# A two-layer backbone on one core: six output blocks with the contraction outside, elementwise work off GpSimd, and new figures for the scheduler

## The chip, the core and the metric

The kernel runs on one core of a Trainium2 chip. A core has a matrix engine (TensorE, PE in the rows), a vector engine (VectorE, DVE), an activation engine (ScalarE, ACT), a general engine (GpSimd, POOL) and a queue engine (SyncE, SP), which here only starts transfers. SBUF is the memory on the core, PSUM its accumulators. The metric is device time in microseconds: the median of repeated executions of the whole program. Shares of time, waits and the clock granted to TensorE (1.0 is 2.4 GHz, 0.5 is 1.2 GHz) come from one profiled execution.

## The reference, cut

Two layers work on 256 latent and 256 context tokens, all float32. `c` gives a modulation of nine vectors for each layer, by one matrix product each.

```python
def swiglu(h, w_gate, w_up, w_down):
    return (jax.nn.silu(h @ w_gate) * (h @ w_up)) @ w_down
def sublayer_in(h, g_pre, mod, s):
    return rmsnorm(h, g_pre) * (1 + mod[:, 3 * s + 1]) + mod[:, 3 * s]
def sublayer_out(h, y, g_post, mod, s, weight):
    return h + weight * mod[:, 3 * s + 2] * rmsnorm(y, g_post)
...
for l in range(DEPTH):
    mod_x = (silu_c @ ada_w[l] + ada_b[l]).reshape(B, N_ADA, 1, D_MODEL)
    mod_c = (silu_cc @ ada_w[l] + ada_b[l]).reshape(1, N_ADA, 1, D_MODEL)
    y = swiglu(sublayer_in(x, norm_pre[l, 0], mod_x, 0), ffn_w_gate[l, 0], ffn_w_up[l, 0], ffn_w_down[l, 0])
    x = sublayer_out(x, y, norm_post[l, 0], mod_x, 0, FFN_RESIDUAL_WEIGHT)
    ...  # the same for ctx; then the mixer (attention and a state space model), then a second FFN
```

The model width is 1024, the FFN's inner width 2816. The last FFN is run for the latent tokens alone.

## The kernel before, in words

**Layout.** Activations lie with channels on the 128 partitions: eight blocks of 128 channels by 512 columns, of which half (h = 0) are context and half (h = 1) latent tokens. Each float32 product is made of three matmuls at the fast rate: weights and activations are split into a high and a low part (`whi`, `wlo`; `hhi`, `hlo`), and high x high, high x low and low x high are added in PSUM (`mm3`). A weight tile `raw` of 128x512 is loaded by SP, its high part made by ACT, its low part by DVE.

**The opening.** `run` loads x, then takes the first two modulation vectors in four quarters (`ada_first`): eight loads `aw` of 256 KB for each quarter, 32 narrow matmuls into 32 partitions, an evacuation `adr` by ACT, a transposition and three small steps on DVE that give the coefficients of two channel blocks. Squares of x go through ones-matmuls into the bank `misc`; `chain` makes the inverse root for each half (rows `rs` of 64 columns on DVE, `sp` the masked rows of 256 columns that a matmul spreads over all partitions). `block` normalises a half of a channel block: `pn` on DVE, `hhi` and again `pn` on ACT, `hlo` on DVE. Then `lead` runs the first six output blocks (three gate/up pairs) for the half h = 0, pair by pair over all eight contraction blocks, and then for h = 1, with 256 columns a matmul. All later blocks have 512 columns.

**Norm changes.** There are five more: FFN to mixer, mixer to FFN and FFN to the next layer's FFN, and the two of layer 1. Each closes the old sublayer (`close`: squares, and the product x times y, together in the tile `tri`, summed by ones-matmuls), makes the factors (`chain`, twice: for the old norm and the new one), and for each block forms `po` = y times the old factor, the sum of x and po, `pn`, `hhi` and `hlo`. Most products `tri` and most sums of x and po run on GpSimd. At the last change (`xonly`, 256 columns, new tiles `xn`) GpSimd also makes the first mask and the products of the first two blocks (EARLY), which read a copy of the factor in SBUF (`b1`).

**What sets the order.** The program records all instructions and a list scheduler orders them before the build: each has a key (the planned TensorE time of the main work before it, plus or minus a shift), a planned duration (`cost`), and a pull towards its kind (TABLE and TILE price a change of ACT's table or TensorE's tile shape). Work aside from the main line (the modulation's rest, the state space model's tables `mt`, `P` and others on DVE) is spread by a pace: PACE_A and PACE_B planned nanoseconds of key for one of DVE. Every instruction is recorded by one helper, so all stand on one line (L576 before, L582 after), and rows are told apart by their tiles.

## Time and profile before

| what | value |
|---|---|
| median of 3 runs | 2302.32 us (2298.68 to 2303.83) |
| profiled execution, its own time | 2301.47 us |
| its span in the trace | 2299.7 us |
| busy: PE, DVE, ACT, POOL | 97%, 81%, 45%, 13% |
| granted clock over the span | 0.988 |
| transfers | 428.06 MB, 186 GB/s on average |

The span is the time between the first and the last instruction of the trace; the execution's own time has 1.8 us more around it. TensorE is nearly always busy, so what counts is where it is not, and where it works at half its clock. An average over the whole run hides this: the table in windows shows it.

### The profile page before, as it was taken

The page shows a single profiled execution, that of the slowest core. Times are in us where ns is not written, and L with a number is a line of the kernel's source. Part 1 is how long each engine was busy: PE and PEld are TensorE (multiplying, and loading weights), DVE is VectorE, ACT ScalarE, POOL GpSimd, SP SyncE. Part 2 cuts the span into 40 slices and gives each one's busy share as a digit, 9 for nine tenths or more (in the row PEclk, how much of TensorE's full clock was granted, in tenths as well). Part 3 has the DMA queues.
Part 4 walks back from the last instruction along what each step waited for, and adds up shares of the span by engine and source line. Part 5 has one row for each costly group of instructions (what it writes and reads, how often), then busy time and mean ns, then how long its engine had stood idle before and what let it go on. Part 6 is the DMA issues. An engine that isn't in the chain of part 4 may idle for free.

```text
span 2299.7 us, 43776 instructions
## 1 busy us (share of the span) xinstructions
PE 2236.4 (97%) x15768; PEld 1926.3 (84%) x15768; DVE 1870.4 (81%) x4314; ACT 1034.4 (45%) x2050; POOL 297.0 (13%) x455
## 2 busy tenths in 40 slices
PE   8999999899999999999999989999999998998998
PEld 6888778787888888888888878888888897997997
DVE  4997878979989889699997999888557579886454
ACT  5332233653347644543222453333246446675452
POOL 0010011330100300200100231110003110312000
PEclk9999999999999999999999989999999999998999
DMA  9344556954975556133554644566444695773552
GB/s 312 102 163 137 172 203 205 359 199 154 319 260 172 170 163 217 48 128 117 176 183 139 210 148 158 200 213 220 152 147 150 236 319 179 186 258 111 179 193 87
DMA packets 237481, 428.06 MB, mean 186 GB/s; under 512 B 29488, under 2 KB 58032, under 8 KB 237264
## 3 DMA queue, kind: packets, MB, share of 16 engines
q1 hardware_dynamic: 213904, 350.79, 47.2%
q0 software_dynamic: 23360, 74.48, 9.2%
q8 instruction: 124, 2.03, 0.4%
q14 instruction: 93, 0.76, 0.1%
HBM read 366.56 MB, written 58.59 MB: 185 GB/s over the span
## 4 chain that ended last, share of the span: by engine, by line
PE 75%; DVE 8%; DMA 3%; issue 1%; ACT 1%; POOL 0%; DVEq 0%; SPq 0%; ACTq 0%; POOLq 0%
PE acc L576 74%; DVE rs L576 1%; DVE t L576 1%; DVE wlo L576 1%; DMA aw<-in_ada_w_dram 1%; PE misc L576 1%; DVE lo L576 1%; DVE w L576 1%; DMA ar<-in_ada_t_dram 0%; DMA m1l<-stg 0%; DMA raw<-in_w_in_dram 0%; DVE po L576 0%; DVE hlo L576 0%; DVE X L576 0%; DVE sp L576 0%
## 5 line engine op out<-in xcount | busy, mean ns | idle before, releaser
L576 PE MATMUL acc<-hhi,whi 128*128 128x256 f32 (+2 forms) x2112 | 717.8, 345 | 5.1 <-ACT hhi L576 4.2
L576 PE MATMUL acc<-hlo,whi 128*128 128x256 f32 (+2 forms) x2112 | 703.9, 344 | 4.8 <-DVE hlo L576 4.8
L576 PE MATMUL acc<-hhi,wlo 128*128 128x256 f32 (+2 forms) x2112 | 706.3, 343 | 0.5 <-DVE wlo L576 0.2
L576 ACT ACTIVATE whi<-raw 128x512 fp32r<-128x512 f32 x802 | 479.0, 624 | 366.7 <-PE acc L576 141.3
L576 DVE TENSOR_TENSOR wlo<-raw,whi 128x512 fp32r<-128x512 f32 x802 | 530.1, 689 | 133.1 <-ACT whi L576 80.3
L576 PEld LDWEIGHTS acc<-hhi,whi 128*128 128x128 f32 (+1 forms) x2112 | 398.7, 190 | 57.2 <-ACT hhi L576 7.0
L576 PEld LDWEIGHTS acc<-hhi,wlo 128*128 128x128 f32 (+1 forms) x2112 | 399.0, 190 | 49.4 <-DVE wlo L576 2.8
L576 PEld LDWEIGHTS acc<-hlo,whi 128*128 128x128 f32 (+1 forms) x2112 | 392.3, 190 | 55.2 <-DVE hlo L576 7.7
L576 PE MATMUL acc<-hi,whi 128*128 128x512 f32 (+1 forms) x1144 | 390.7, 344 | 2.4 <-DVE lo L576 2.0
L576 PE MATMUL acc<-lo,whi 128*128 128x512 f32 (+1 forms) x1144 | 388.6, 341 | 0.0
L576 PE MATMUL acc<-hi,wlo 128*128 128x512 f32 (+1 forms) x1144 | 384.2, 343 | 1.0 <-DVE wlo L576 1.0
L576 PEld LDWEIGHTS acc<-hi,whi 128*128 128x128 f32 x1144 | 215.3, 189 | 32.3 <-DVE lo L576 2.4
L576 PEld LDWEIGHTS acc<-hi,wlo 128*128 128x128 f32 x1144 | 214.4, 189 | 27.8 <-DVE wlo L576 2.2
L576 PEld LDWEIGHTS acc<-lo,whi 128*128 128x128 f32 x1144 | 215.5, 189 | 25.0 <-issue 0.9
L576 ACT ACTIVATE sg<-acc 128x512 f32<-128x512 f32 (+1 forms) x129 | 64.9, 504 | 231.5 <-PE acc L576 212.9
L576 ACT ACTIVATE hi<-sg 128x512 fp32r<-128x512 f32 (+1 forms) x113 | 60.6, 542 | 167.9 <-DVE sg L576 142.2
L576 DVE TENSOR_TENSOR sg<-sg,acc 128x512 f32<-128x512 f32 (+1 forms) x97 | 55.7, 575 | 97.0 <-ACT sg L576 62.0
L576 POOL TENSOR_TENSOR tri<-x,y 128x256 f32<-128x256 f32 x54 | 52.4, 976 | 320.5 <-ACT y L576 299.0
L576 POOL DMA_DIRECT2D stg<-P x64 | 34.8, 543 | 376.7 <-DVE P L576 360.9
L576 DVE CUSTOM_DVE_ANT_0 ar<-ar,crow,adab 128x512 f32<-128x512 f32 x104 | 79.0, 760 | 3.6 <-DMA ar<-in_ada_t_dram 3.4
L576 DVE CUSTOM_DVE_ANT_0 ar<-ar,crow,ah 128x512 f32<-128x512 f32 x104 | 79.0, 759 | 2.0 <-DMA ar<-in_ada_t_dram 1.1
L576 DVE TENSOR_TENSOR lo<-sg,hi 128x512 fp32r<-128x512 f32 (+1 forms) x113 | 65.6, 586 | 16.9 <-ACT hi L576 10.8
(249 smaller groups left out, 3234.5 us busy)
## 6 DMA issues: line engine op xcount, KB each, us to landing
raw<-in_w_gu_dram SPq DMA_DIRECT2D x352, 256.0 KB, 3.2
ar<-in_ada_t_dram SPq DMA_DIRECT2D x208, 256.0 KB, 3.5
raw<-in_w_dn_dram SPq DMA_DIRECT2D x176, 256.0 KB, 3.1
raw<-in_w_sq_dram SPq DMA_DIRECT2D x128, 256.0 KB, 4.3
raw<-in_w_in_dram SPq DMA_DIRECT2D x112, 256.0 KB, 5.2
m1l<-stg SPq DMA_DIRECT2D x96, 256.0 KB, 5.1
aw<-in_ada_w_dram SPq DMA_DIRECT2D x80, 256.0 KB, 5.8
stg<-P POOLq DMA_DIRECT2D x64, 256.0 KB, 3.4
```

The lines of the kernel that those rows point to most:

```text
L576: getattr(getattr(self.tc.nc, engine), method)(*[real(v) for v in a], **{k: real(v) for k, v in kw.items()})
```

## The change

- The first FFN of layer 0 gets its own `lead_first`: all six blocks are open at once, in six banks; for each quarter of the modulation the two channel blocks are normalised in both halves, and each of them runs through all six blocks with 512 columns a matmul. The weights come in halves: the six for contraction blocks 0 to 3 ahead of quarter 0, the other six ahead of quarter 2. `with self.rec.at(...)` gives loads a fixed key (FIRST for the modulation's quarters, FIRST_W for the weights), which sets SP's order.
- The inverse root of both halves is made in one go of 128 columns (`open`), into one bank; `keep` copies both factors to SBUF after the first quarter. The transposition of a quarter uses the other part of that quarter's bank.
- No product or sum is left on GpSimd: `tri`, the sums, the last change's products and mask are DVE's. The copy `b1` and EARLY go. GpSimd keeps its transfers and small clears.
- Planned durations change: matmuls, the scan, a transfer started by GpSimd, its landing, TILE from 90 to 180. PACE_B goes from 2.5 to 3.2.

```diff
-PACE_A, PACE_B = 1.6, 2.5
+PACE_A, PACE_B = 1.6, 3.2
...
-FIRST = (5000, 1000, 1000, 1000)
+FIRST, FIRST_W = (1, 3, 4, 6), (2, 5)
...
-    TABLE, TILE = 1283, 90
+    TABLE, TILE = 1283, 180
...
-            return 1038 if eng == "POOL" else 525
+            return 545 if eng == "POOL" else 525
...
-            if m < 128:
-                return 28 + max(n, m) * passes * m / 307.2
-            return 2.5 + max(n * passes / 2.4, 53.3 * min(passes, 2) * (1 if method == "transpose" else 2))
+            if m < 128 and passes > 1:
+                return 6 + n * passes * m / 307.2
+            return (13.5 if passes == 1 else 4) + n * passes / 2.4
...
+        if method == "tensor_tensor_scan":
+            return 67 + 2.083 * n
...
-                    dma = max(dma, op.end + self.DMA_IN + 1000 * (e == "POOL")) + op.bytes / 360.0
+                    dma = max(dma, op.end + self.DMA_IN + 1400 * (e == "POOL")) + op.bytes / 360.0
...
-            nc.gpsimd.tensor_tensor(xy, x, y, op=ALU.mult)
+            nc.vector.tensor_tensor(xy, x, y, op=ALU.mult)
...
+    def lead_first(self, nrm, evac, first):
+        nc = self.nc
+        mine = self.chunks[self.i_get:self.i_get + 2 * LEAD]
...
+        bank, ws = [], [[None, None] for _ in range(LEAD)]
+        next(first)
+        for q in range(4):
+            if q % 2 == 0:
+                for i in range(LEAD):
+                    r = self.rec.tile("slot", 512, F32, "raw")
+                    with self.rec.at(FIRST_W[q // 2]):
+                        nc.sync.dma_start(r, mine[2 * i + q // 2][0])
+                    ws[i][q // 2] = r
+            with self.rec.ahead(URGENT):
+                for k in (2 * q, 2 * q + 1):
+                    self.rec.urgent = k == 0
+                    for h in (0, 1):
+                        nrm.block(h, k)
+            self.rec.urgent = False
+            if q == 0:
+                nrm.keep()
+            for k in (2 * q, 2 * q + 1):
+                for i in range(LEAD):
+                    if k == 0:
+                        bank.append(self.acc())
+                    if k % 4 == 0:
+                        ws[i][q // 2] = self.split(ws[i][q // 2], 512, self.blk(512, F32R, "whi"),
+                                                   self.blk(512, F32R, "wlo"))
+                    self.mm3(bank[i], ws[i], k, nrm.h[k], k == 0, k == NB - 1)
+                if k % 2 == 0:
+                    next(first, None)
+        for j in range(LEAD // 2):
+            evac(j, bank[2 * j], bank[2 * j + 1])
...
-            e.tensor_tensor(t, T.part(self.y[i], h), b1, op=ALU.mult)
-            (nc.vector if i < 2 and not self.xonly else nc.gpsimd).tensor_tensor(xv, xo, t, op=ALU.add)
+            nc.vector.tensor_tensor(t, T.part(self.y[i], h), b1, op=ALU.mult)
+            nc.vector.tensor_tensor(xv, xo, t, op=ALU.add)
```

Two places show the new order. The first is TensorE in the opening, at its first weight matmuls: `aw` are the modulation's loads, `hhi` and `hlo` the parts of a normalised channel block, `whi` and `wlo` those of a weight tile, each `acc` a bank. Before:

```order
L576 MATMUL acc_392<-aw_289,c_70 32x128 x4
L576 MATMUL acc_429<-hhi_413,whi_357 128x256
L576 MATMUL acc_429<-hhi_413,wlo_373 128x256
L576 MATMUL acc_429<-hhi_413,whi_377 128x256
L576 MATMUL acc_429<-hhi_413,wlo_383 128x256
L576 MATMUL acc_392<-aw_299,c_70 32x128 x4
L576 MATMUL acc_392<-aw_315,c_70 32x128 x4
L576 MATMUL acc_429<-hlo_440,whi_357 128x256
```

And after, at the change from the second to the third quarter:

```order
L582 MATMUL acc_485<-hhi_539,wlo_487 128x512
L582 MATMUL acc_625<-aw_356,c_70 32x128 x4
L582 MATMUL acc_625<-aw_367,c_70 32x128 x4
L582 MATMUL acc_625<-aw_372,c_70 32x128 x4
L582 MATMUL acc_625<-aw_380,c_70 32x128 x4
L582 MATMUL acc_625<-aw_386,c_70 32x128 x4
L582 MATMUL acc_625<-aw_391,c_70 32x128 x4
L582 MATMUL acc_625<-aw_399,c_70 32x128 x4
L582 MATMUL acc_625<-aw_407,c_70 32x128 x4
L582 MATMUL acc_397<-hhi_557,whi_343 128x512
L582 MATMUL acc_397<-hlo_579,whi_343 128x512
```

The modulation's narrow matmuls stood between those of one pair of blocks; now a quarter's 32 stand together, between two channel blocks that each go through six banks.

The second place is DVE at the last norm change, from the last masked rows `sp` on. Before:

```order
L576 SCALAR_TENSOR_TENSOR sp_25539<-rs_25544,sp_25539 128x256
L576 TENSOR_TENSOR po_25550<-y_25234,acc_25519 128x256
L576 TENSOR_TENSOR po_25554<-y_25279,acc_25519 128x256
L576 TENSOR_TENSOR po_25558<-y_25346,acc_25519 128x256
L576 TENSOR_TENSOR pn_25560<-xn_25542,acc_25552 128x256
L576 TENSOR_TENSOR pn_25564<-xn_25547,acc_25552 128x256
```

After:

```order
L582 SCALAR_TENSOR_TENSOR sp_25341<-rs_25344,sp_25341 128x256
L582 TENSOR_TENSOR po_25348<-y_24976,acc_25327 128x256
L582 TENSOR_TENSOR po_25352<-y_25014,acc_25327 128x256
L582 TENSOR_TENSOR xn_25354<-x_84,po_25348 128x256
L582 TENSOR_TENSOR xn_25356<-x_85,po_25352 128x256
L582 TENSOR_TENSOR pn_25358<-xn_25354,acc_25350 128x256
L582 TENSOR_TENSOR pn_25360<-xn_25356,acc_25350 128x256
```

The products of the third to fifth block stood between `sp` and the first `pn`; now the products and sums of the first two blocks stand there, which GpSimd had made beside the chain.

## Rows read from the trace of the kernel before

**Rows 1.** The page, busy time of each engine, share of the span, instructions:

```profile
PE 2236.4 (97%) x15768; PEld 1926.3 (84%) x15768; DVE 1870.4 (81%) x4314; ACT 1034.4 (45%) x2050; POOL 297.0 (13%) x455
```

**Rows 2.** Windows of the opening: length; PE, PEld, DVE, ACT, POOL busy; PEclk, DMA, GB/s:

```profile
10.00:15.00 5.00, 3.94 (x104) 2.00 (x96) 1.19 (x11) 2.82 (x9) 0.00 (x0) 1.00 1.08 369
...
20.00:25.00 5.00, 4.16 (x45) 2.12 (x44) 4.97 (x17) 2.79 (x6) 0.00 (x0) 0.50 1.10 348
25.00:30.00 5.00, 5.00 (x57) 3.27 (x52) 0.69 (x4) 0.88 (x2) 0.00 (x0) 0.73 1.09 356
...
60.00:65.00 5.00, 5.00 (x43) 5.00 (x43) 4.93 (x15) 3.12 (x7) 0.00 (x0) 1.00 0.28 93
```

**Rows 3.** Timeline of PE in the opening: start, time, instruction and its count:

```profile
22.98 0.58 PE L576 MATMUL acc<-hhi,whi 128*128 128x256 f32 x1
...
43.39 1.08 PE L576 MATMUL acc<-aw,c 128*32 128x128 f32 x32
...
70.85 0.39 PE L576 MATMUL acc<-hlo,whi 128*128 128x512 f32 x1
```

**Rows 4.** Timeline of SP, which starts the transfers:

```profile
0.74 0.94 SPq L576 DMA_DIRECT2D aw<-in_ada_w_dram  x2
1.74 0.46 SPq L576 DMA_DIRECT2D cvec<-in_cvec_dram  x1
...
3.19 3.75 SPq L576 DMA_DIRECT2D x<-in_x_dram  x8
```

**Rows 5.** Timeline of ACT in the opening, with the idle time before and its releaser:

```profile
6.82 1.39 ACT L576 ACTIVATE sq<-x 128x256 f32<-128x256 f32 x4 [0.43 <-DMA x<-in_x_dram]
...
46.47 0.59 ACT L576 ACTIVATE hhi<-pn,c,cA 128x256 fp32r<-128x256 f32 x1
```

**Rows 6.** Windows of 50 us over the whole run, columns as in rows 2:

```profile
400.00:450.00 50.00, 45.85 (x605) 39.74 (x594) 46.28 (x102) 32.51 (x72) 20.20 (x33) 1.00 1.02 386
450.00:500.00 50.00, 47.01 (x403) 43.41 (x402) 49.46 (x143) 33.20 (x72) 16.69 (x23) 1.00 0.49 152
...
1350.00:1400.00 50.00, 44.68 (x333) 41.81 (x334) 47.91 (x125) 27.64 (x57) 13.55 (x20) 0.90 0.34 116
...
1600.00:1650.00 50.00, 50.00 (x222) 41.42 (x221) 28.67 (x60) 13.88 (x24) 0.00 (x0) 1.00 0.49 162
...
2050.00:2100.00 50.00, 40.40 (x354) 37.37 (x353) 40.24 (x95) 31.02 (x69) 17.32 (x15) 0.89 0.50 160
```

**Rows 7.** Groups of POOL: shapes, count, busy us and mean ns, idle before and releasers:

```profile
L576 POOL TENSOR_TENSOR tri<-x,y 128x256 f32<-128x256 f32 x54 | 52.4, 976 | 320.5 <-ACT y L576 299.0 <-PE misc L576 7.0 <-issue 6.7
L576 POOL TENSOR_TENSOR x<-x,po 128x256 f32<-128x256 f32 x48 | 40.8, 863 | 64.1 <-DVE po L576 59.5 <-ACT y L576 4.2
```

**Rows 8.** Timelines of DVE, then POOL, at the last norm change:

```profile
2087.98 0.23 DVE L576 TENSOR_TENSOR rs<-rs 128x64 f32<-128x64 f32 x1
2088.24 0.49 DVE L576 SCALAR_TENSOR_TENSOR rs<-rs,rs 128x64 f32<-128x64 f32 x2
...
2092.29 0.98 DVE L576 SCALAR_TENSOR_TENSOR rs<-rs,rs 128x64 f32<-128x64 f32 x2
2093.30 0.65 DVE L576 TENSOR_TENSOR rs<-rs 128x64 f32<-128x64 f32 x1
2093.87 0.95 DVE L576 TENSOR_TENSOR sp<-rs,ident 128x256 f32<-128x256 f32 x1
2094.75 0.73 DVE L576 TENSOR_TENSOR rs<-rs,rs 128x64 f32<-128x64 f32 x1
...
2096.35 1.07 DVE L576 TENSOR_TENSOR po<-y,acc 128x256 f32<-128x256 f32 x3
...
2092.46 1.41 POOL L576 TENSOR_TENSOR po<-y,b 128x256 f32<-128x256 f32 x2 [3.00 <-ACT b L576]
```

**Rows 9.** Groups of DVE, columns as in rows 7:

```profile
L576 DVE TENSOR_TENSOR hlo<-pn,hhi 128x256 fp32r<-128x256 f32 x88 | 40.8, 468 | 4.8 <-ACT pn L576 4.5
...
L576 DVE TENSOR_TENSOR pn<-x,acc 128x256 f32<-128x256 f32 x80 | 31.4, 412 | 6.7 <-ACT pn L576 4.2 <-PE acc L576 2.3
```

More of the change, by code (lines that the diff above doesn't have):

```diff
@@ L272, in ahead, with at @@
         return self.aside(-ns)
+    def at(self, key):
+        return self.aside(key - self.now - self.shift)
     def cost(self, eng, method, a, kw):
@@ L717, in stat, with rsqrt @@
             self.nc.tensor.matmul(out, self.ones, q[:, :, j], start=False, stop=False, skip_group_check=True)
-    def rsqrt(self, v, plain=False, wide=True, times=1.0, mask=None):
+    def rsqrt(self, v, plain=False, wide=True, times=1.0):
         nc = self.nc
         end = 1.875 * times
-        mask = mask or nc.vector
         n = v.shape[-1]
@@ L735, in rsqrt @@
             r = self.blk(256, name="sp").rearrange("p (j k) -> p j k", j=4)
-            mask.tensor_tensor(r, y[:, c:c + 64].unsqueeze(1).to_broadcast([128, 4, 64]), diagonal, op=ALU.mult)
+            nc.vector.tensor_tensor(r, y[:, c:c + 64].unsqueeze(1).to_broadcast([128, 4, 64]), diagonal, op=ALU.mult)
             rows.append(r)
@@ L842, in ada_first @@
         for q in range(4):
-            bank = self.acc()[:, 0:128]
+            full = self.acc()
+            bank = full[:, 0:128]
+            self.rec.pull = FIRST_PULL
             for kt in range(8):
@@ L846, in ada_first @@
                 src = self.io["ada_w"][0, kt * 128:(kt + 1) * 128, 0:2048].rearrange("p (m c) -> p m c", m=2)
-                with self.rec.ahead(FIRST[q]):
+                with self.rec.at(FIRST[q]):
                     nc.sync.dma_start(w.rearrange("p (m c) -> p m c", m=2), src[:, :, q * 256:q * 256 + 256])
@@ L854, in ada_first @@
             nc.scalar.activation(row, bank, AF.Copy)
-            tp = self.aux()[:, 0:128]
+            tp = full[:, 128:256]
             nc.tensor.transpose(tp, row, self.ident)
@@ L955, in gated, with ffn @@
         nc.vector.tensor_tensor(out[1], sg, _f(out[0]), op=ALU.subtract)
-    def ffn(self, l, f, nrm, nxt):
+    def ffn(self, l, f, nrm, nxt, first=None):
         nc = self.nc
@@ L964, in ffn, with evac @@
         g = {}
-        self.lead(nrm, self.gate_half(g, n))
+        if first is None:
+            self.lead(nrm, self.gate_half(g, n))
+        else:
+            def evac(j, pg, pu):
+                g[j] = self.blk(n, F32R, "hi"), self.blk(n, F32R, "lo")
+                self.gated(self.blk(n, name="sg"), pg, pu, g[j])
+            self.lead_first(nrm, evac, first)
         hh = nrm.h
@@ L1944, in run @@
         nc.vector.memset(self.ones, 1.0)
-        self.ve = [self.const([128, 64], name="ve") for _ in range(2)]
+        ve = self.const([128, 128], name="ve")
+        self.ve = [ve[:, 64 * h:64 * h + 64] for h in range(2)]
         self.mods = [self.const([128, 144]) for _ in range(L)]
@@ L1979, in run @@
             nc.vector.memset(self.region(3 * h), 0.0)
-            nrm.chain(h)
-        for _ in first:
-            pass
+        nrm.open(ve)
         self.rot = ld([128, 128], io["rot"], "rot")
@@ L2010, in to_next @@
                 return Norm(self, (l, 2), (l + 1, 0), y, False)
-            nrm = self.ffn(l, 0, nrm, to_mixer)
+            nrm = self.ffn(l, 0, nrm, to_mixer, first if l == 0 else None)
             nrm = self.mixer(l, xo, nrm, to_ffn2)
@@ L2045, in chain @@
         T.rec.urgent = self.xonly or RUSH
-        mask = T.nc.gpsimd if self.xonly else None
         b1, b2 = self.banks()
         self.bc[h] = T.flat(b1), T.flat(b2)
-        if self.post is not None:
-            w = T.blk(64, name="rs")
-            v.tensor_scalar(w, T.region(3 * h), D * EPS, None, op0=ALU.add)
-            st = T.region(3 * h + 1, 2)
-            if not self.xonly:
-                st = T.blk(128, name="rs")
-                v.tensor_copy(st, T.region(3 * h + 1, 2))
-                v.memset(T.region(3 * h, 3), 0.0)
-            r, rows = T.rsqrt(w, True, times=D ** 0.5, mask=mask)
-            T.spread(b1, rows[0])
-            if self.xonly:
-                self.b1 = T.flat(T.blk(256, name="b1"))
-                T.nc.scalar.activation(self.b1, T.flat(b1), AF.Copy)
-            a = T.blk(64, name="rs")
-            v.tensor_tensor(a, r, st[:, 0:64], op=ALU.mult)
-            v.scalar_tensor_tensor(a, st[:, 64:128], 2.0, a, op0=ALU.mult, op1=ALU.add)
-            v.tensor_tensor(a, a, r, op=ALU.mult)
-            v.tensor_tensor(T.ve[h], T.ve[h], a, op=ALU.add)
+        w = T.blk(64, name="rs")
+        v.tensor_scalar(w, T.region(3 * h), D * EPS, None, op0=ALU.add)
+        st = T.region(3 * h + 1, 2)
+        if not self.xonly:
+            st = T.blk(128, name="rs")
+            v.tensor_copy(st, T.region(3 * h + 1, 2))
+            v.memset(T.region(3 * h, 3), 0.0)
+        r, rows = T.rsqrt(w, True, times=D ** 0.5)
+        T.spread(b1, rows[0])
+        a = T.blk(64, name="rs")
+        v.tensor_tensor(a, r, st[:, 0:64], op=ALU.mult)
+        v.scalar_tensor_tensor(a, st[:, 64:128], 2.0, a, op0=ALU.mult, op1=ALU.add)
+        v.tensor_tensor(a, a, r, op=ALU.mult)
+        v.tensor_tensor(T.ve[h], T.ve[h], a, op=ALU.add)
         w = T.blk(64, name="rs")
@@ L2070, in chain, with open, keep @@
         T.rec.urgent = False
+    def open(self, ve):
+        T = self.T
+        T.rec.urgent = True
+        bank = T.acc()
+        w = T.blk(128, name="rs")
+        T.nc.vector.tensor_scalar(w, ve, D * EPS, None, op0=ALU.max)
+        for h, r in enumerate(T.rsqrt(w, times=D ** 0.5)[1]):
+            T.spread(bank[:, 256 * h:256 * h + 256], r)
+            self.bc[h] = None, T.flat(bank[:, 256 * h:256 * h + 256])
+        T.rec.urgent = False
+    def keep(self):
+        for h in range(2):
+            b = self.T.flat(self.T.blk(256, name="fb"))
+            self.T.nc.scalar.activation(b, self.bc[h][1], AF.Copy)
+            self.bc[h] = None, b
     def block(self, h, i):
```

11 lines of the change are left out of this document (7 added, 4 removed).

## The prediction

> **What bounds the kernel now.** I began with the page's busy shares: TensorE is busy for 2236.4 of 2299.7 us [rows 1], so 63.3 us of idle time are all that a better order can win, beside stretches in which it works at a low granted clock and beside the work itself. Then the table in windows of 50 us [rows 6]: a steady stretch shows 222 matmuls of 512 columns in 50.00 us, 0.2252 us each, with nothing idle. The idle time sits at the opening and at the changes from one norm to the next: 4.2 and 3.0 us between 400 and 500, 5.3 between 1350 and 1400, 9.6 between 2050 and 2100. In the first three of these windows DVE is busy for 46.28 to 49.46 of 50 us: there DVE is late, not TensorE. The reader is to see in the opening's windows [rows 2] that the DMA engines are full (a share of 1.08 to 1.10, 348 to 369 GB/s) while TensorE waits or runs at half speed: a granted clock of 0.50 from 20 to 25 us and 0.73 from 25 to 30, so in these ten microseconds 3.9 us are lost to the clock alone. TensorE's own rows [rows 3] give the ends of the opening: the first weight matmul at 22.98 us, the first 512-column one, with which the first six output blocks are over, at 70.85.
>
> **The opening.** Before, the six blocks are 288 matmuls of 256 columns; 43 of these stand in 5 us at full clock [rows 2], 0.116 us each, 33.5 us. Now they are 144 of 512 columns, 144 x 0.2252 = 32.4 us: 1.1 us of pure work is gone. More is in when they may run. The order rows show that each quarter of the contraction now feeds all six blocks and both halves of the columns as soon as a quarter of the modulation is there, where before the first half of the columns ran through all eight contraction blocks and the second half followed.
>
> The transfers set one floor. Ahead of the last quarter's matmuls stand 8 of x, 32 of the modulation's weights and 12 halves of the first six blocks, 52 transfers of 256 KB. At 360 GB/s [rows 2] one takes 0.73 us. The loads of x now follow three small ones; these took 1.74 to 3.19 us before, 1.45 us, so x is issued from about 2.2 us instead of 3.19 [rows 4]. The first one was in use 3.6 us after its issue [rows 4, 5], so now at 5.8, and the 52nd lands at 5.8 + 51 x 0.73 = 43.0. From the last of these matmuls to the first normalised block it took 43.39 to 46.47, 3.1 us [rows 3, 5]; two more activations and the second half's pass are some 1.2 us; then 36 matmuls of 0.2252 us, 8.1. Floor by transfers: 55.4 us.
>
> TensorE sets the other. Its first weight matmul needs the same 16 transfers (x and one quarter) and the same chain as before, so it starts at about 22.5, near the 22.98 of before. From there: 32.4 us of weight matmuls; three quarters of the modulation, 96 matmuls, of which 32 took 1.08 us [rows 3], 3.2 us; and the 3.9 us of low clock, which I leave as they are, since the first quarter still waits for weights to be split. That is 62.0. The same sum for before, 22.98 + 33.5 + 3.2 + 3.9 = 63.6, falls 7.3 us short of the 70.85 measured; the rest was waits and changes between narrow and wide matmuls. Now the modulation's matmuls stand in solid groups, so I expect a fifth of that rest, 1.5 us, and take 63.5: **7.3 us** gained. The bounds are 55.4 (15.4 gained) and 62.0 + 7.3 = 69.3 (1.5 gained). I take a value near TensorE's own sum because it is the later of the two floors. What comes next is a steady stretch of 512-column matmuls at full occupation, so the gain is carried on, up to the next place where DVE is late.
>
> The copy of the row factors to SBUF (two activations) lies on ACT while it waits for data, and frees a bank; I cost it at nothing. One thing may be late: on ACT the evacuation of the last quarter's modulation now stands behind an exponential's table load and splits of three later weight tiles. These tiles are some 7 transfers further, 5 us, so the evacuation may slip to about 49 us; TensorE then still has the third quarter's matmuls to run. Without that cover it would cost up to 5 us, which is inside the bounds.
>
> **GpSimd's arithmetic on DVE.** 54 products tri and 48 sums x leave GpSimd, where one took 0.98 and 0.86 us [rows 7], and with them, at the last norm change, 8 sums, 2 products and a mask (so many by the code): 113 instructions. On DVE three such products in a row took 1.07 us for the first 0.41 and two more [rows 8], 0.33 us each, so DVE gets 37.7 us more, about 8 at each of the first four norm changes and 5 to 6 at the last. Against it stands what GpSimd takes from DVE while it runs. In the last norm change two products of 64 columns took 0.49 us when GpSimd was idle and 0.98 while it multiplied; single products of 64 columns took 0.65 and 0.73 there and the mask of 256 columns 0.95, against 0.23 and some 0.41 undisturbed [rows 8]: 0.49 + 0.42 + 0.50 + 0.54 makes 1.9 us lost in a chain on which TensorE waits, while GpSimd did its two products and the two sums behind them. Over the whole run the same is seen in the mean: the subtraction hlo, of the same size as pn but with both inputs in SBUF, took 468 ns against 412 [rows 9]. So 113 instructions off GpSimd give DVE back between nothing and 113 x 0.48 = 54 us (1.9 us by four instructions); I take 34, near the rows of the chain but with the tri products, which run beside PSUM work, giving less. DVE's load at a norm change then grows by 0 to 3 us, while each link that went through GpSimd gets 0.4 to 0.6 us shorter.
>
> At the last norm change the chain is urgent and nothing else is on DVE, so nearly all of the 1.9 us comes off directly; the mask that GpSimd had made beside it costs 0.1 of it. The products and sums of the first two blocks now stand on DVE, 4 x 0.33 = 1.3 us, in the gap between the second factor's rows (sp) and the first pn, in which DVE already did three products of 1.07 us [rows 8]; hence **1.8 us** gained, bounds 0 and 4 (the second with the low clock that such a wait leaves). At the other four I take **3 us** in all, bounds 12 lost and 11 gained (half of the 22 us of idle time in the three worst windows and the last).
>
> Here a rule speaks against the change. The Trainium skill, "Perfetto Trace Analysis", section "Optimizing Scalar/DVE Operations", says that with DVE saturated, moving work to other engines, even GpSimd, may make sense, and adds that the two share a read port, so that it might not help. The change goes the other way at stretches where DVE is saturated. By the first half of the rule the norm changes get longer (the third rival); rows 8 side with the second half.
>
> **The scheduler's figures.** The planned cost of a 512-column matmul rises from 215.9 to 226.8 ns, against 225.2 measured [rows 6]; the planned cost of a DMA issue on GpSimd falls to the measured size. Work that is due by planned TensorE time (the state space model's tables on DVE) so comes about 5% earlier against TensorE's true time, and what of it piled up on DVE at 400 us is smaller. PACE_B of 3.2 thins the same work in layer 1. I put no separate gain on this; it is why the 3 us above are not a loss. All else is a new order of equal work, worth between -5 and +5 us.
>
> **Sum.** The profiled execution took 2301.47 us, 0.85 below the median of 2302.32, so no correction: 2301.5 - 7.3 - 1.8 - 3.0 = 2289.4, **2289 us**.
>
> **Rivals.**
> 1. *More is freed.* The opening comes down near the transfers' floor (12 us) and the norm changes lose half of their idle time (11) with the clock they waste (3): 2301.5 - 26 = 2275. For it: those windows wait on DVE rows that GpSimd slowed. Against it: DVE is busy for 49.46 of 50 us from 450 on [rows 6] and sheds nothing. Chance 0.17.
> 2. *The clock takes the opening's gain.* Between quarters TensorE now waits for the next quarter's data. If the clock falls to 1.2 GHz at each wait, as in 20 to 25 us [rows 2], the first two quarters (16 us at full clock) need up to 16 us more; half of it eats the 7.3, and 2297 to 2301 remain. Against it: by the sums above TensorE is the later one from 30 us on, so it does not wait. The Trainium skill, "TensorE: Matmul & The Clock Gate", section "HAM oscillation — how this bites in real kernels", describes a kernel that falls back to the low clock at every contraction tile since each tile's data is waited for. No row here shows it after 30 us. Chance 0.15 together with other ways to stay within 0.2%: DVE's new load giving back what the opening gave (2302).
> 3. *DVE becomes later: slower.* If GpSimd's absence gives DVE little back, each saturated norm change (400 to 500, 1300 to 1400) grows by its 24 x 0.33 = 8 us, the two others by half: 24 us. Less 7.3 and 1.8: 2301.5 + 14.9 = 2316. It decides against the change from where less than 24 of the 37.7 us come back. Rows 8 show more coming back than is added (0.48 us for 0.33 an instruction). Chance 0.09.
>
> **How the numbers follow.** About 0.2% is what a measurement of this kernel can tell from no change, 4.6 us: faster means under 2297.7, slower over 2306.9. The forecast (2281 to 2297) has 0.59, rival 1 0.17, rivals 2 and 3 0.15 and 0.09. Faster 0.77, same 0.14, slower 0.09; 0.01 of rival 2 lies below its limit. The range reaches to rival 1's time and to no change: 2274 to 2302. It leaves out 0.09 of rival 3, about 0.05 of rival 2 and about 0.05 of rival 1.
>
> **What would show it.** The first 512-column matmul of the seventh block at 61 to 66 us; granted clock 1.0 from 30 us on; DVE's hlo at about 415 ns and its 64-column rows at 0.23 us in every norm change; the last wait on sp shorter by 1.8 us; TensorE idle in 400 to 500 at or under 7 us. Wrong would be: the seventh block after 68 us, TensorE waiting longer on DVE around 400 and 1350, or a new wait on weights where DVE's splits come late.

## The result, and the profile after

The changed kernel takes **2273.74 us** (median of 4 runs, 2269.72 to 2279.49), the kernel before 2300.5 beside it (4 runs, 2296.01 to 2303.83): a ratio of 0.9889, 95% interval 0.9876 to 0.9901, so 26.8 us less. The forecast was 2289, with a range that began at 2274: right in direction, less than half of the gain, and just outside the range. The profiled execution of the changed kernel is the slowest of its four (2279.49), so the two traces are 22.0 us apart and not 26.8.

The page of the changed kernel, busy time (against [rows 1]):

```profile
PE 2226.1 (98%) x15624; PEld 1909.5 (84%) x15624; DVE 1872.8 (82%) x4412; ACT 1031.5 (45%) x2045; POOL 195.7 (9%) x342
```

DVE is busy for 2.4 us more than before, near the prediction's account (37.7 added, 34 given back). GpSimd has lost 101 us, and TensorE's idle time fell from 63.3 to 51.6 us.

Windows of the changed kernel, columns as in [rows 2] and [rows 6] (busy time of each engine and, in brackets, its instructions):

```profile
20.00:25.00 5.00, 1.20 (x3) 0.92 (x4) 3.99 (x13) 3.96 (x10) 0.00 (x0) 0.86 1.04 342
25.00:30.00 5.00, 5.00 (x32) 2.62 (x32) 5.00 (x13) 3.61 (x8) 0.00 (x0) 0.50 1.09 347
30.00:35.00 5.00, 5.00 (x57) 3.83 (x56) 0.26 (x2) 0.28 (x1) 0.00 (x0) 0.96 1.08 368
...
400.00:450.00 50.00, 45.02 (x610) 39.76 (x610) 31.02 (x80) 30.00 (x69) 9.17 (x17) 0.97 1.02 374
450.00:500.00 50.00, 48.01 (x419) 45.15 (x418) 49.96 (x166) 33.64 (x74) 3.68 (x5) 1.00 0.49 149
950.00:1000.00 50.00, 49.45 (x378) 46.05 (x377) 49.96 (x167) 30.33 (x63) 0.00 (x0) 1.00 0.36 116
1350.00:1400.00 50.00, 49.38 (x299) 43.95 (x298) 50.00 (x121) 21.49 (x42) 1.89 (x4) 1.00 0.54 180
2050.00:2100.00 50.00, 42.16 (x358) 39.44 (x357) 37.43 (x97) 30.80 (x65) 0.00 (x0) 0.90 0.33 102
```

In 1350 to 1400 TensorE now idles for 0.6 us where it idled for 5.3, and at a granted clock of 1.00 where it was 0.90 [rows 6]. DVE is busy for the whole of that window, and TensorE hardly waits for it. From 950 to 1000 it idles for 0.6 us; the kernel before had 2.6 there, and a clock of 0.93:

```profile
950.00:1000.00 50.00, 47.41 (x378) 45.64 (x377) 47.62 (x153) 33.83 (x70) 11.44 (x13) 0.93 0.30 94
```

In 400 to 450 nothing was gained: most of the 5.0 us of idle time there are now waits for the modulation's transfers (4.7 us between 400 and 500, shown with the tile price below).

Since the work is reordered, windows of equal time hold different work. The table below therefore compares the times at which both kernels have the same share of their weight matmuls' columns behind them, worked out from all TensorE rows of the two traces: the lead of the changed kernel, and how much of it is idle time, other matmuls, and weight matmuls that took longer than 0.2252 us for 512 columns (low clock, change of shape).

| time in the kernel before | lead | idle | other matmuls | slow weight matmuls |
|---|---|---|---|---|
| 100 (after the opening) | 3.2 | -2.1 | 2.9 | 2.4 |
| 500 | -0.3 | -4.8 | 2.7 | 1.7 |
| 900 | 5.9 | 0.7 | 3.0 | 2.2 |
| 1050 | 9.9 | 2.8 | 3.3 | 3.8 |
| 1400 | 26.5 | 9.1 | 9.1 | 8.2 |
| 1650 | 18.9 | 6.5 | 6.3 | 6.1 |
| 2050 | 20.3 | 9.9 | 5.5 | 4.9 |
| 2150 | 22.0 | 11.7 | 6.0 | 4.3 |

Between 900 and 1650 lie 13.0 of the 22.0 us: two norm changes, at 950 and at 1300 to 1400 (of the 16.6 won there, 7.6 go back by 1650, in all three columns). The opening gave 3.2, but at 500, behind the first norm change, the changed kernel has no lead left; the last norm change gave 1.7.

TensorE in the opening of the changed kernel (start, time, instruction; in square brackets the idle time before it and what ended that; against [rows 3]):

```profile
24.12 0.79 PE L582 MATMUL acc<-hhi,whi 128*128 128x512 f32 x1 [3.42 <-ACT hhi L582]
...
52.96 1.96 PE L582 MATMUL acc<-aw,c 128*32 128x128 f32 x64
...
67.39 0.39 PE L582 MATMUL acc<-hhi,whi 128*128 128x512 f32 x1
```

From 24.12 to 67.39, the first matmul after the 144, TensorE waits for nothing. A quarter of the modulation, 32 matmuls, is 64 records in 1.96 us.

The last norm change, from the first `rs` row on DVE to the first weight matmul on TensorE, in the kernel before and then in the changed one:

```profile
2087.49 0.23 DVE L576 TENSOR_SCALAR rs<-misc 128x64 f32<-128x64 f32 x1 [0.84 <-PE misc L576]
2099.05 0.58 PE L576 MATMUL acc<-hhi,whi 128*128 128x256 f32 x1 [1.28 <-ACT hhi L576]
```

```profile
2067.07 0.22 DVE L582 TENSOR_SCALAR rs<-misc 128x64 f32<-128x64 f32 x1 [0.83 <-PE misc L582]
2074.08 1.19 PE L582 MATMUL acc<-sp,c 128*128 128x256 f32 x2 [3.15 <-DVE sp L582]
2076.42 0.58 PE L582 MATMUL acc<-hhi,whi 128*128 128x256 f32 x1 [1.15 <-ACT hhi L582]
```

Between them, DVE of the changed kernel (against [rows 8]):

```profile
2071.77 0.48 DVE L582 SCALAR_TENSOR_TENSOR rs<-rs,rs 128x64 f32<-128x64 f32 x2
2072.29 0.23 DVE L582 TENSOR_TENSOR rs<-rs 128x64 f32<-128x64 f32 x1
2072.43 0.42 DVE L582 TENSOR_TENSOR sp<-rs,ident 128x256 f32<-128x256 f32 x1
```

The rows that GpSimd had stretched to 0.98, 0.65 and 0.95 us take 0.48, 0.23 and 0.42, and the whole stretch 9.35 us in place of 11.56. In the traces of the six runs below that have other combinations of the change's parts it is the same: 9.34 to 9.35 us in the three without arithmetic on GpSimd, 11.49 to 11.55 in the three with it.

### The profile page after: what moved, and what is told of

Same layout as the page of the kernel before. It is cut to its first block, busy times and chain, and to the rows that moved or that the text cites. A ratio compares the mean times of both kernels' runs of the same rounds, so it can differ in the third digit from the quotient of the medians.

```text
span 2277.7 us, 43323 instructions
## 1 busy us (share of the span) xinstructions
PE 2226.1 (98%) x15624; PEld 1909.5 (84%) x15624; DVE 1872.8 (82%) x4412; ACT 1031.5 (45%) x2045; POOL 195.7 (9%) x342
## 5 line engine op out<-in xcount | busy, mean ns | idle before, releaser
L582 PE MATMUL acc<-hhi,whi 128*128 128x512 f32 (+1 forms) x2064 | 709.7, 348 | 9.3 <-ACT hhi L582 7.3
L582 PE MATMUL acc<-hhi,wlo 128*128 128x512 f32 (+1 forms) x2064 | 703.3, 346 | 0.1
L582 PE MATMUL acc<-hlo,whi 128*128 128x512 f32 (+1 forms) x2064 | 699.2, 347 | 0.7 <-DVE hlo L582 0.7
L582 PEld LDWEIGHTS acc<-hhi,whi 128*128 128x128 f32 x2064 | 388.2, 189 | 64.5 <-ACT hhi L582 11.7
L582 PEld LDWEIGHTS acc<-hhi,wlo 128*128 128x128 f32 x2064 | 388.1, 189 | 53.4 <-DVE wlo L582 5.5
L582 PEld LDWEIGHTS acc<-hlo,whi 128*128 128x128 f32 x2064 | 383.6, 189 | 50.7 <-DVE hlo L582 1.8
L582 DVE TENSOR_TENSOR lo<-sg,hi 128x512 fp32r<-128x512 f32 (+1 forms) x110 | 63.8, 584 | 20.8 <-ACT hi L582 11.7
L582 DVE TENSOR_TENSOR y<-y,acc 128x512 f32<-128x512 f32 (+1 forms) x96 | 52.3, 546 | 18.9 <-PE acc L582 18.8
```

Of the source, the lines that this page charges most:

```text
L582: getattr(getattr(self.tc.nc, engine), method)(*[real(v) for v in a], **{k: real(v) for k, v in kw.items()})
```

## The experiments

The change has three parts: the opening (O), the work off GpSimd (G), the planner's figures with the tile price and the pace (S). The first six runs have every other combination of them; their edits are pieces of the diff ahead of the prediction, applied or taken back whole. Two theories stand against each other. By A the gain is G's, since DVE is no longer slowed. By B it is the order that S's figures make. Differences below are between medians, against the kernel before of the same session or the 2273.74 of the changed kernel. The median of the kernel before lay between 2299.2 and 2300.5 in all sessions. The changed kernel's own runs spread over 10 us and its interval is some 2.9 us to either side, so a difference from it of 3 or 4 us is not told from none.

**G alone** (`tri`, sums, last change on DVE; the rest as before).

> The kernel before with one part of the change: no product, sum or mask on GpSimd, all on DVE; opening and planned durations as before. Theory A (the norm changes gain because DVE is no longer slowed by GpSimd): most of the gain is here, 12 to 18 us less than the kernel before, TensorE idle at 950 to 1000 and 1300 to 1400 down by some 8 us in all, and the last change 1.8 us shorter. Theory B (the gain comes from the new planned durations, which order the work at the norm changes better): 2 to 5 us less, mostly at the last change. By the prediction's own sum: 4.8 us less.

Measured: 2285.34, ratio 0.9932 (0.9919 to 0.9946), **15.0 us less**. Theory A by the time, and the last change is 2.2 us shorter. The idle time did not do what A said: from 950 to 1000 and from 1300 to 1400 it fell from 10.5 to 9.5 us in all, not by 8. At equal work 9.6 us of the trace's lead arise between 900 and 1400, of which 5.2 are weight matmuls that are less slow and 1.1 idle time; 6.9 are there by 500.

**O alone** (`lead_first`, `open`, `keep`, `at`).

> The kernel before with the new opening alone; GpSimd's arithmetic and planned durations as before. Both theories: the first 512-column matmul of the seventh block comes 4 to 7 us earlier, the whole 3 to 7 us less. By the prediction's sum: 7.3 us less. If the opening's part is lost again where DVE is late next (400 to 500 us), it is 0 to 2.

Measured: 2294.14, ratio 0.9978 (0.9970 to 0.9987), 6.2 us less. In the trace the seventh block begins at 67.20, some 3.7 us earlier than in the kernel before, a little under the 4 to 7 expected.

**S alone.**

> The kernel before with the new planned durations, the larger tile price and the pace of 3.2 alone; opening and GpSimd's arithmetic as before. Theory A: between 3 us more and 3 us less. Theory B: 10 to 18 us less, with less idle time of TensorE at 1300 to 1400. The prediction gave this no gain of its own (between -5 and +5 us).

Measured: 2297.62, ratio 0.9989 (0.9980 to 0.9998), 2.7 us less. Theory A.

**Without G.**

> The changed kernel with products, sums and the first mask back on GpSimd, as before; the new opening and the new planned durations stay. Theory A (DVE freed from GpSimd makes the gain): 12 to 18 us above the changed kernel, with TensorE's idle time at the norm changes back. Theory B (the planned durations make it): 2 to 5 us above it.

Measured: 2295.37, ratio 0.9982 (0.9973 to 0.9992): **21.6 us above** the changed kernel, more than A had said.

**Without O.**

> The changed kernel with the old opening; the other two parts stay. Both theories: 3 to 7 us above the changed kernel. By the prediction's sum: 7.3 above it.

Measured: 2276.87, ratio 0.9897 (0.9884 to 0.9911): 3.1 us above the changed kernel; the intervals overlap.

**Without S.**

> The changed kernel with the old planned durations, tile price and pace; the new opening and the work off GpSimd stay. Theory A: within 3 us of the changed kernel. Theory B: 10 to 18 us above it. A third case: the figures matter only together with the work on DVE (their pace thins DVE's side work where DVE now has the products and sums as well), then this one is well above the changed kernel although the figures alone gave the kernel before nothing.

Measured: 2283.16, ratio 0.9922 (0.9909 to 0.9936): 9.4 us above the changed kernel, the third case. In all four settings G takes off 11.0 to 21.6 us (mean 17.1) and O 2.2 to 6.2 (mean 3.4). S gives between 1.2 more and 9.4 less. So most of the change's gain is G's, 15.0 of the 26.8 us by itself, and the prediction had it at 4.8 us.

Then what G's gain is made of: A1, DVE's speed beside GpSimd; A2, the shorter way without GpSimd in it.

**Idle work on GpSimd** (the changed kernel; DVE still makes what is used; 208 of 256 columns, as much as room was left for).

```diff
+            nc.gpsimd.tensor_tensor(self.flat(self.scr), x[:, :, 0:26], y[:, :, 0:26], op=ALU.mult)
             nc.vector.tensor_tensor(xy, x, y, op=ALU.mult)
...
+            if i >= 2 and not self.xonly:
+                nc.gpsimd.tensor_tensor(T.flat(T.scr), T.part(self.y[i], h)[:, :, 0:26], t[:, :, 0:26], op=ALU.add)
             nc.vector.tensor_tensor(xv, xo, t, op=ALU.add)
```

> The changed kernel, and beside it GpSimd makes each product and each sum that it made in the kernel before (those at the first four norm changes, 208 of the 256 columns) once more, into a tile that nobody reads. DVE still makes the ones that are used, so no link goes through GpSimd; only its reading beside DVE is back. Theory A1 (the gain of the work off GpSimd is DVE's undisturbed speed): DVE's rows are slowed by some 25 to 35 us again, on top of the arithmetic it now has, and the time rises by 12 us or more over the changed kernel, to 2286 or above. Theory A2 (the gain is the shorter link: no way through GpSimd's 0.86 and 0.98 us and its signals): DVE's rows are slowed as well, but the time stays within 4 us of the changed kernel.

Measured: 2297.86, ratio 0.9988 (0.9979 to 0.9997): **24.1 us above** the changed kernel, for work whose result nobody reads; in the trace no other engine waits for it. In the listings 26 of DVE's and 21 of TensorE's instructions stand in another place than in the changed kernel. Its page, then groups of DVE, first of the changed kernel, then of this one (count, busy us, mean ns):

```profile
PE 2234.1 (97%) x15624; PEld 1910.7 (83%) x15624; DVE 1904.5 (83%) x4412; ACT 1032.2 (45%) x2045; POOL 278.4 (12%) x444
```

```profile
L582 DVE TENSOR_TENSOR hlo<-pn,hhi 128x256 fp32r<-128x256 f32 x88 | 36.3, 413 | 3.8 <-ACT pn L582 3.6
L582 DVE TENSOR_TENSOR pn<-x,acc 128x256 f32<-128x256 f32 x68 | 27.0, 406 | 1.4 <-ACT whi L582 0.9 <-ACT fb L582 0.5
L582 DVE TENSOR_TENSOR x<-x,po 128x256 f32<-128x256 f32 x64 | 25.8, 411 | 0.0
```

```profile
L582 DVE TENSOR_TENSOR hlo<-pn,hhi 128x256 fp32r<-128x256 f32 x88 | 40.4, 459 | 3.4 <-ACT pn L582 3.3
L582 DVE TENSOR_TENSOR x<-x,po 128x256 f32<-128x256 f32 x64 | 34.1, 541 | 0.0
L582 DVE TENSOR_TENSOR pn<-x,acc 128x256 f32<-128x256 f32 x68 | 27.0, 407 | 2.9 <-ACT whi L582 2.5 <-ACT fb L582 0.5
```

The sum of two SBUF tiles goes from 411 to 541 ns, `hlo` from 413 to 459, and `pn`, whose second input is a bank of PSUM, stays at 407. Within this trace, the 32 sums that overlap a GpSimd instruction take 0.67 us on the mean and the 32 that don't 0.41; of `pn`, 15 and 53 take 0.41 both. The Trainium skill, "SBUF — State Buffer", section "Who interferes with whom", says that a DVE instruction with two inputs in SBUF contends with a GpSimd one that reads SBUF, and that one with at most one input there does not, outside DVE's 2-port modes. These three groups agree with it. A group with a single SBUF input was slowed here all the same, the step ahead of the second inverse root; whether it runs in such a mode no row shows (changed kernel, then this one):

```profile
L582 DVE TENSOR_SCALAR rs<-ve 128x64 f32<-128x64 f32 x9 | 1.7, 184 | 0.0
L582 DVE TENSOR_SCALAR rs<-ve 128x64 f32<-128x64 f32 x9 | 3.2, 354 | 0.0
```

DVE's busy time grew by 31.7 us and the whole by 24.1, so 0.76 us for each (within some 0.1, by the changed kernel's interval).

**Sums alone, and products alone, back on GpSimd.**

> The changed kernel with the 48 sums of x and po back on GpSimd; the products tri and the last change stay on DVE. Theory A1: a loss by GpSimd's busy time, 41 of the 100 us, some 6 to 8 us above the changed kernel. Theory A2: most of the loss, 10 us or more, since each sum lies between po and pn.

> The changed kernel with the 54 products tri back on GpSimd; the sums and the last change stay on DVE. Theory A1: some 8 to 10 us above the changed kernel. Theory A2: under 4 us, since only the last product of a norm change lies on the path to the factors.

Measured: 2287.72 (0.9948, 0.9936 to 0.9961), **14.0 us above** the changed kernel, and 2283.70 (0.9931, 0.9918 to 0.9945), **10.0 above**. Both are above what A1 said or at its end, and the products far over A2's 4 us. Their pages, sums first:

```profile
PE 2232.4 (98%) x15624; PEld 1911.7 (84%) x15624; DVE 1871.4 (82%) x4364; ACT 1031.5 (45%) x2045; POOL 238.3 (10%) x390
```

```profile
PE 2226.7 (98%) x15624; PEld 1909.8 (84%) x15624; DVE 1871.0 (82%) x4358; ACT 1031.9 (45%) x2045; POOL 245.7 (11%) x396
```

DVE's busy time is that of the changed kernel to 2 us, and the time is 10 to 14 us longer. So DVE's total is not what decides. Either the way through GpSimd does (A2), or a microsecond by which DVE is slowed costs more than a microsecond of arithmetic. Both kernels are new plans, so these sizes hold what another order is worth as well.

**The pace.**

```diff
-PACE_A, PACE_B = 1.6, 3.2
+PACE_A, PACE_B = 1.6, 2.5
```

> The changed kernel with the pace of layer 1 back at 2.5; all planned durations stay. If the pace makes what the new figures gave (9 us on the changed kernel), it lies 6 to 9 us above the changed kernel; if the planned durations and the tile price make it, within 3 us.

Measured: 2270.98, ratio 0.9878 (0.9865 to 0.9892): 2.8 us *below* the changed kernel, inside the spread of its runs. No gain of the pace is shown.

**Idle work on DVE** (as the idle GpSimd work, with `nc.vector`, and planned at 1 ns).

> The changed kernel, and DVE itself makes the 102 products and sums of the run before last but three (GpSimd's idle work) a second time, into the tile that nobody reads; GpSimd makes none. The planner counts them at nothing, so the order of the rest stays nearly that of the changed kernel. They are worth 102 x 0.28 = 29 us of DVE, all undisturbed, against the 31.7 us by which GpSimd's idle work lengthened DVE's busy time. Theory A1 (at a norm change each microsecond of DVE counts, whether by arithmetic or by GpSimd's reading): 18 to 26 us above the changed kernel, the idle and low-clock places being the same as with GpSimd's idle work. In that case the arithmetic that the change gave to DVE cost about as much, and the gain must come from the links that no longer go through GpSimd. Theory A3 (GpSimd's reading does more than lengthen DVE's instructions): 10 us or less above the changed kernel.

Measured: 2291.19, ratio 0.9967 (0.9955 to 0.9979): **17.5 us above** the changed kernel, just under A1's bounds. Page:

```profile
PE 2236.2 (98%) x15624; PEld 1911.5 (84%) x15624; DVE 1901.3 (83%) x4514; ACT 1031.2 (45%) x2045; POOL 195.2 (9%) x342
```

DVE's 28.5 us more cost 0.61 us each, near the 0.76 of the slowing by GpSimd. What a microsecond on DVE costs at a norm change, if the plan doesn't know of it, is about the same whether it is arithmetic or interference. The comparison is rough: here 103 of DVE's and 100 of TensorE's instructions stand in another place, more than with the idle GpSimd work.

**Old matmul figures.**

```diff
-            if m < 128 and passes > 1:
-                return 6 + n * passes * m / 307.2
-            return (13.5 if passes == 1 else 4) + n * passes / 2.4
+            if m < 128:
+                return 28 + max(n, m) * passes * m / 307.2
+            return 2.5 + max(n * passes / 2.4, 53.3 * min(passes, 2) * (1 if method == "transpose" else 2))
...
-        if method == "tensor_tensor_scan":
-            return 67 + 2.083 * n
```

> The changed kernel with the old planned durations of matmuls and of the scan; the tile price of 180, the transfers' figures and the pace of 3.2 stay. If the matmuls' figures make the 9 us that the figures together gave on the changed kernel, it lies 6 to 10 us above it; if the tile price makes them, within 3 us.

Measured: 2289.46, ratio 0.9953 (0.9940 to 0.9965): 15.7 us above the changed kernel, more than all old figures together gave (9.4).

**A link without the reading.**

```diff
             nc.vector.tensor_tensor(xv, xo, t, op=ALU.add)
+            if i >= 2 and not self.xonly:
+                for _ in range(5):
+                    nc.gpsimd.tensor_copy(xv[:, 0, 0:8], xv[:, 0, 0:8])
```

> The changed kernel with a link through GpSimd but without its reading: after each of the 48 sums DVE has made, GpSimd copies 8 of its 256 columns onto themselves five times, and the product pn on DVE waits for the last of these copies. DVE makes all arithmetic; GpSimd reads 40 columns' worth where a sum read 512. Theory A2 (the time of the link through GpSimd makes the gain, while what DVE gets back and what it gets more cancel): 6 us or more above the changed kernel, with DVE's rows hardly slowed. Theory A1 (DVE's slowing where it is late makes it all): under 3 us above it.

Measured: 2277.31, ratio 0.9903 (0.9890 to 0.9917): 3.6 us above the changed kernel, between the two and nearer to A1. GpSimd's row, then DVE's `hlo`:

```profile
L582 POOL COPY x<-x 128x8 f32<-128x8 f32 x240 | 62.5, 293 | 255.1 <-DVE x L582 249.8
```

```profile
L582 DVE TENSOR_TENSOR hlo<-pn,hhi 128x256 fp32r<-128x256 f32 x88 | 36.8, 419 | 4.8 <-ACT pn L582 4.7
```

Five copies are 1.3 us by the group's busy time (62.5 / 48), longer than the 0.863 of a real sum [rows 7], and `hlo` stays at 419 ns. A way through GpSimd of that length is worth some 4 us of the sums' 14, if that can be told from another order at all. That speaks against A2 as the main cause; the orders kept, below, do so without a new plan.

**The tile price.**

```diff
-    TABLE, TILE = 1283, 180
+    TABLE, TILE = 1283, 90
```

> The changed kernel with the price of a change of TensorE's tile shape back at 90; all planned durations and the pace of 3.2 stay. If the new price belongs to the figures' gain: more changes of shape and 3 to 8 us above the changed kernel. If the matmuls' planned durations alone make it: within 3 us.

Measured: **2258.78**, ratio 0.9819 (0.9805 to 0.9832): 15.0 us *below* the changed kernel. Neither case: the price that the change doubled costs it 15 us. TensorE's waits from 400 to 500 us (us in total, times, longest), changed kernel, then this one; then this one's windows:

```profile
PE acc L582 <- DMA aw<-in_ada_w_dram: 4.7, 3, 3.3
PE acc L582 <- ACT hhi L582: 1.4, 1, 1.4
```

```profile
PE acc L582 <- ACT hhi L582: 0.9, 1, 0.9
```

```profile
400.00:450.00 50.00, 49.88 (x655) 44.53 (x646) 39.57 (x117) 36.26 (x84) 5.37 (x10) 1.00 1.00 356
450.00:500.00 50.00, 49.06 (x353) 45.90 (x352) 46.27 (x142) 27.00 (x58) 8.93 (x13) 1.00 0.56 192
```

In this run TensorE no longer waits for the modulation's weights at 400 us. By the comparison at equal work, 12.7 of its lead over the changed kernel are there at 500 us, 9.0 of them idle time. That is where the gain lies. The loads themselves start earlier: by SP's rows the last 20 of the modulation's loads are issued from 389.12 to 412.01 us here, and the last 19 of the changed kernel's from 399.33 to 422.95. What the price is meant for does not explain it: at the higher price the changed kernel changes TensorE's tile shape more often, not less, 198 times against 183 by their matmul rows.

**Orders kept.** What is left is whether G's effect is the chip's or only the planner's luck with another order. In these two kernels all engines' orders are those of the changed kernel and of the kernel before; only the engine that executes the 102 instructions is another. The edit to the changed kernel (that to the kernel before is its mirror, with `Engine(self, "vector", "POOL")`):

```diff
+        self.other = Engine(self, "gpsimd", "DVE")
...
-            nc.vector.tensor_tensor(xy, x, y, op=ALU.mult)
+            nc.other.tensor_tensor(xy, x, y, op=ALU.mult)
...
-            nc.vector.tensor_tensor(xv, xo, t, op=ALU.add)
+            (nc.vector if i < 2 or self.xonly else nc.other).tensor_tensor(xv, xo, t, op=ALU.add)
```

> The changed kernel with every engine's order kept to the instruction: the 54 products and the 48 sums are planned as DVE's and stand where they stood, but GpSimd executes them. Theory M (the gain of the work off GpSimd is a mechanism of the chip: GpSimd's reading and the way through it): 12 us or more above the changed kernel. Theory P (it is the planner's luck: other durations, other order): under 5 us above it, since the order is the same.

> The kernel before with every engine's order kept: the 54 products and 48 sums are planned as GpSimd's, but DVE executes them at that place of the whole order. Theory M: 8 us or more less than the kernel before, although the plan knows nothing of DVE's new work. Theory P: between 4 us less and some us more, as DVE's arithmetic comes where the plan had put none.

Measured: 2289.06 (0.9956, 0.9943 to 0.9968), **15.3 us above** the changed kernel, and 2295.37 (0.9979, 0.9970 to 0.9988), **4.8 below** the kernel before. Pages, in that order:

```profile
PE 2233.3 (98%) x15624; PEld 1911.2 (84%) x15624; DVE 1875.4 (82%) x4310; ACT 1031.9 (45%) x2045; POOL 280.3 (12%) x444
```

```profile
PE 2235.0 (97%) x15768; PEld 1924.3 (84%) x15768; DVE 1873.2 (82%) x4416; ACT 1033.3 (45%) x2050; POOL 203.0 (9%) x353
```

In the order made for DVE's work, GpSimd's part costs 15.3 us by the chip alone: theory M. In the trace of this run `hlo` takes 504 ns, against 413 in the changed kernel, and other engines wait for GpSimd for 1.1 us in all, 0.9 of it DVE's `pn` (us in total, times, longest):

```profile
L583 DVE TENSOR_TENSOR hlo<-pn,hhi 128x256 fp32r<-128x256 f32 x88 | 44.4, 504 | 6.0 <-ACT pn L583 5.6
DVE pn L583 <- POOL x L583: 0.9, 3, 0.3
```

So with the order held it is the slowing of DVE (A1), and hardly the way through GpSimd (A2). By their traces these two kernels lie only 9.6 us apart, since the changed kernel's is its slowest run; 5.6 of these are weight matmuls that took longer, 2.4 idle time. In the order made for GpSimd's work, taking it off gives 4.8, between the two theories. G alone, which differs from the second by a new plan and by the 11 instructions of the last change, gave 15.0. Of the 10.2 us between the two some 2 are the last change's; the other 8 came with the order that is planned for the work where it is done.

**A price that means nothing, and two edits together** (`TILE` 175; `TILE` 90 and `PACE_B` 2.5).

> The changed kernel with the tile price at 175 in place of 180, an edit that means nothing by itself but gives another order. If the price works by what it says, the time stays within 2 us of the changed kernel. If any new order moves the time as far as the tile price of 90 did (15 us less), then it moves here by 5 us or more to either side, and the 3 to 10 us that the figures and the opening are worth in the other runs can't be put down to a cause.

> The changed kernel with the tile price at 90 and the pace at 2.5, both as in the kernel before; the planned durations stay new. If the two edits add up: 2256 us (2258.8 with the price of 90 alone, less the 2.8 that the pace alone gave). If what they give is a matter of the order as a whole: anywhere between 2256 and 2275.

Measured: 2269.64 (0.9864, 0.9849 to 0.9879), 4.1 us below the changed kernel, and 2259.25 (0.9820, 0.9807 to 0.9834), as with the price of 90 alone. In the listings the edit to 175 moves 416 of DVE's and 513 of TensorE's instructions. Its interval overlaps with the changed kernel's, so what such an edit is worth lies between nothing and some 4 us by this one case; the 15 us of the price of 90 show that an order can be worth more. The 2 to 6 us of the opening and the 3 to 4 of the pace and of the link can't be told from that by their size. The price of 90 gave 14.5 to 15.0 in both runs that had it with the new figures; the 15.7 of the old matmul figures is one run. The changed kernel with the price of 90 is the fastest version found, 41.7 us under the kernel before.

## Why the prediction was right and wrong

**The opening: right in kind, 7.3 predicted, 3.2 measured** in the trace and 2.2 to 6.2 in the runs. By its terms: the first weight matmul came at 24.12 and not at 22.5. The 144 matmuls with their low clock took 36.6 us against 36.3. The three quarters of the modulation took 6.6 us against 3.2. Waits and the rest took 0.1 against 1.5. The step that failed is the modulation: the row of 1.08 us in [rows 3] holds 32 records, and I took them for a quarter; a quarter is 64, so 3.4 us were missing. The same mistake made the "rest" of the kernel before look like 7.3 us of waits, where by its rows 4.3 of it was the modulation. TensorE was the later floor, as predicted, and the clock was back at 0.96 in 30 to 35 us and stayed, against rival 2. Its sentence that no row shows a fall of the clock after 30 us holds for the opening; at the norm changes [rows 6] show 0.90 and 0.89. The gain was not carried on as the prediction had it: the changed kernel has no lead at 500 us. In the run with the opening alone 4.7 us of lead are there at 500, so the loss is not the opening's; the waits for the modulation's loads at 400 us come in its place.

**The last norm change: right**, mechanism and size. 1.8 predicted; from the first `rs` row on DVE to the first weight matmul it takes 9.35 us (2067.07 to 2076.42) where it took 11.56 (2087.49 to 2099.05), 2.2 less, and so in the three other runs of the first six that have G.

**The other norm changes: wrong in size**, 3 us predicted, some 13 in the trace; it is rival 1's time (2275) that came, but not its split, which had 12 us at the opening. The balance on DVE was right: its busy time grew by 2.4 us where the prediction had 3.7 (113 x 0.33 is 37.3 and not 37.7, which changes nothing). The step that failed is the sentence that netted the two into 0 to 3 us more of DVE's load at a norm change, and the 3 us taken from it, as if a microsecond of arithmetic and one of slowing cost the same. In before, G alone, sums alone, products alone, both kept orders and after, DVE is busy for 1870.4 to 1875.4 us, and their times run from 2274 to 2301. With the order kept, the same 102 instructions cost 15.3 us more on GpSimd than on DVE, for 2.6 us of difference in DVE's busy time. A slowing is in no planned duration, comes in the middle of the norm changes, and costs 0.76 us a microsecond (idle GpSimd work), about as arithmetic that the plan does not know (0.61, idle DVE work). Arithmetic that the plan knows can be placed among the other work. The planned kind was not measured by itself; that it costs clearly less is inferred from G alone (15.0 less) against the kept order (4.8 less), of which some 2 are the last change's. For these 102 instructions the sum had 3.0, near the 4.8 of the kept order of before; it left out what a plan for the new order makes of them.

**The rule against the change** lost: DVE was saturated, and taking the work off GpSimd onto DVE gave 11.0 to 21.6 us. By the Trainium skill, "Perfetto Trace Analysis", section "Optimizing Scalar/DVE Operations", the two engines share an SBUF read port and the offload might not help; in the order kept, the offload to GpSimd cost 15.3 us.

**The figures: wrong as a zero.** They give 2.7 alone and 9.4 with the rest, of which another order can be a good part, and inside them the tile price costs 15. Why the matmul figures and the price act so strongly against each other is open. The runs show where (the modulation's transfers at 400 us, issued 10 us later), not by which decision of the planner.

**What was to be seen:** the seventh block at 67.39 and not at 61 to 66; clock 0.96 in 30 to 35 and 1.0 behind it; `hlo` at 413 ns and the 64-column `rs` rows at 0.18 to 0.22 us on the mean; the last change 2.2 us shorter; TensorE idle in 400 to 500 at 7.0 us, but for another reason, the modulation's weights.

## To carry to other kernels

Before giving work to GpSimd, sum how much longer DVE's instructions run beside it, those with two SBUF inputs above all, and where: here 102 instructions of under a microsecond each were worth 15 us in an unchanged order made without them, and 5 in one made for them. Equal busy time on an engine is no equal cost; a delay that the schedule doesn't know is the dear kind, as far as these runs tell. Where a planner sets the order, shift one of its figures by a few per cent to see how far the time moves without a reason (up to 4 us here for a price of 175 in place of 180), and try each figure of a bundle alone (one of them cost 15).

## What was not expected of the hardware

An fp32 matmul into 32 partitions shows as two records: 32 instructions of a quarter are 64 rows. A GpSimd copy of 8 columns takes 293 ns, a third of a product of 256 columns (976 ns, [rows 7]), and five in a row beside DVE left `hlo` at 419 ns. Work on GpSimd whose result nobody uses cost 24.1 us of 2274.
